# A mixture-of-experts kernel: the load of b1 moved to the head of SyncE's opening loads

## The chip, the cores and the metric

The kernel runs on one core of one Trainium2 chip. The metric is the device time of one execution in microseconds (us), so lower is better.

## The reference

Eight experts each run a two-layer network on their own 256 tokens. x is 8 x 256 x 512, w1 is 8 x 512 x 2048, w2 is 8 x 2048 x 512, all fp32; b1 is 8 x 2048 and b2 is 8 x 512.

```python
h = np.matmul(x, w1) + b1[:, np.newaxis, :]
h = np.maximum(h, 0)
return (np.matmul(h, w2) + b2[:, np.newaxis, :]).astype(np.float32)
```

## The kernel before

**Sizes and precision.** Each expert has 4 MB of w1 and 4 MB of w2 in fp32. Both are cast to fp16 by the DMAs that load them, so 2 MB of each arrive on the chip. `w1_sb` and `w2_sb` hold three experts (`NW` = 3), `xT` holds the transposed x of four (`NX` = 4), and `hT` holds the hidden layer of four (`NH` = 4).

**The two stages of the program.** First come `first_loads` and `first_turns`, whose waits are derived automatically from the data that the instructions share. Then comes a critical section, in which each engine has a program written out by hand with its own semaphores (`run_gpsimd`, `run_sync`, `run_scalar`, `run_vector`, `run_tensor`). SyncE, ScalarE, VectorE and TensorE enter the section at one wait for everything that the first stage started: the loads of both queues and the work of every engine. GpSimd passes the same wait only at line 180, after it has issued the loads of w1 of experts 1 and 2 (line 163), so those two loads lie ahead of it.

**The opening loads.** `first_loads` issues four loads from SyncE's queue (line 347) in the order of a tuple: x of expert 0 into `pair0` (512 KB), x of expert 1 into `pair1` (512 KB), b1 into `b1_rows` (64 KB, as 32 partitions of 512 fp32), and x of experts 2 and 3 into the first half of `outg0` (1 MB). GpSimd's queue gets w1 of expert 0 and b2 (line 352).

**The opening turns.** `first_turns` prepares three things:
- the identity matrix. GpSimd fills a scratch `steps` (lines 356 to 359), VectorE transposes it (line 360), and ScalarE copies four blocks into `ident` (line 363);
- the transposed x of experts 0 and 1. ScalarE casts them to fp16 (line 365), TensorE transposes them against `ident` (line 372), and ScalarE copies the result out of PSUM into `xT` (line 373);
- the transposed bias `b1T`, with four transposes on VectorE that read `b1_rows` (line 375).

On VectorE the four bias transposes are issued ahead of the transpose of `steps`, though they stand later in the source. On ScalarE the order is the two casts, the four copies into `ident`, then the two copies into `xT`.

**The critical section.** For 11 steps, TensorE runs the first layer of expert s (line 288) and then the second layer of expert s - 3 (bias at line 303, matmuls at line 318). ScalarE first casts x of experts 2 and 3 (line 195), and VectorE transposes them (line 222). ScalarE evicts the first layer with bias and ReLU (line 106); ScalarE, and VectorE for the last two experts, evict the second (line 118). SyncE waits for each load of w1 and w2 to land and then tells TensorE (lines 145 and 151). GpSimd issues the weight loads in one fixed order: w1 of expert s at line 163, then w2 of expert s - 3 at line 171, with x of experts 4 to 7 at line 177. From expert 3 on, a load waits until TensorE has finished with the buffer that it reuses. The results of experts 0 to 5 leave through GpSimd's queue (line 187), the last two through SyncE's (lines 155 and 389).

Of the kernel before, what the change touches and what calls it, by code (L numbers as in the profile page):

```python
# [10 lines left out]
def kernel(  # L11
# [20 lines left out]
    nB = P // B  # L32
# [15 lines left out]
    def sb(name, shape, dt=fp16):  # L48
        return nc.alloc_sbuf_tensor(name, shape, dt).ap()
# [10 lines left out]
    b1_rows = sb("b1rows", [E * nB, M // nB], fp32)  # L60
# [71 lines left out]
    def w1_of(e):  # L132
        return w1[e].rearrange("(p kc) m -> p kc m", kc=nKC)

    def x_of(first):
        n = FIRST[first]
        return x[first : first + n].rearrange("e (p r) h -> (e p) r h", r=n * nTB)
# [201 lines left out]

    def first_loads():  # L340
        for to, rows in (
            (x32[0], x_of(0)),
            (x32[1], x_of(1)),
            (b1_rows, b1.rearrange("e (b i) -> (e b) i", b=nB)),
            (x32[2], x_of(2)),
        ):
            tc.keep_in_program_order(nc.sync.dma_start(out=to, in_=rows))  # L347
        for to, rows in (
            (w1_sb[:, 0], w1_of(0)),
            (b2_sb, b2.rearrange("e h -> (e h)").rearrange("(o f) -> o f", o=1)),  # L350
        ):
            tc.keep_in_program_order(nc.gpsimd.dma_start(out=to, in_=rows))

    def first_turns():
# [19 lines left out]
        for b in range(nB):  # L374
            v.transpose(  # L375
                out=b1T[b * B : (b + 1) * B, nB - 1 - b : nB - 1 - b + nJ * B],
                in_=b1_rows.rearrange("r (i j) -> r j i", j=nJ))

    first_loads()
    first_turns()  # L380
    with tc.tile_critical(sync_engine=mybir.EngineType.Pool, no_gpsimd_drain=True):
# [45 lines left out]
```

## Time and profile before

| what | value |
|---|---|
| time, median of 3 runs | 180.99 us (180.72 to 181.39) |
| the profiled execution's own time | 180.8 us |
| its span, first to last instruction | 179.0 us |
| TensorE matmuls, busy | 130.6 us (73%) |
| ScalarE, busy | 86.3 us (48%) |
| VectorE, busy | 37.8 us (21%) |
| DMA, moved | 40.98 MB, mean 229 GB/s |
| HBM | read 71.39 MB, written 4.19 MB |
| landing of the b1 load after its issue | 7.5 us |

All times in the views count from the start of the span. The profiled execution took 1.8 us more than its span. DMA bytes are counted as written: a weight load that casts fp32 to fp16 reads two bytes for each byte that it moves by this count. PE is TensorE, DVE is VectorE, ACT is ScalarE, POOL is GpSimd and SP is SyncE; a trailing q names the engine's queue of commands. "x2" in a row counts instructions.

### The profile page before, as it was taken

The page shows a single profiled execution, that of the slowest core. Times are in us where ns is not written, and L with a number is a line of the kernel's source. Part 1 is how long each engine was busy: PE and PEld are TensorE (multiplying, and loading weights), DVE is VectorE, ACT ScalarE, POOL GpSimd, SP SyncE. Part 2 cuts the span into 40 slices and gives each one's busy share as a digit, 9 for nine tenths or more (in the row PEclk, how much of TensorE's full clock was granted, in tenths as well). Part 3 has the DMA queues.
Part 4 walks back from the last instruction along what each step waited for, and adds up shares of the span by engine and source line. Part 5 has one row for each costly group of instructions (what it writes and reads, how often), then busy time and mean ns, then how long its engine had stood idle before and what let it go on. Part 6 is the DMA issues. An engine that isn't in the chain of part 4 may idle for free.

```text
span 179.0 us, 2880 instructions
## 1 busy us (share of the span) xinstructions
PE 130.6 (73%) x800; PEld 86.5 (48%) x800; DVE 37.8 (21%) x39; ACT 86.3 (48%) x160; POOL 13.4 (7%) x30
## 2 busy tenths in 40 slices
PE   0004299596969993999956996699669997998940
PEld 0003278585858641786446644584268433443410
DVE  0092299300000299991000000000000000001010
ACT  3304658585858606674089705980398213121010
POOL 7100000302020101001010001000200001002000
PEclk9999999999999999579999999999999999999997
DMA  6999989999999998998999999899899999999995
GB/s 211 272 260 269 234 183 227 234 205 207 234 216 194 234 231 179 234 234 190 220 234 205 205 234 220 190 234 234 176 234 234 198 212 205 220 227 198 334 453 238
DMA packets 3825, 40.98 MB, mean 229 GB/s; under 512 B 448, under 2 KB 464, under 8 KB 1136
## 3 DMA queue, kind: packets, MB, share of 16 engines
q0 software_dynamic: 3056, 37.76, 95.2%
q1 hardware_dynamic: 768, 3.21, 4.6%
q14 instruction: 1, 0.01, 0.0%
HBM read 71.39 MB, written 4.19 MB: 422 GB/s over the span
## 4 chain that ended last, share of the span: by engine, by line
DMA 37%; PE 33%; ACT 16%; DVE 6%; issue 3%; SPq 1%; POOL 0%; ACTq 0%
PE po L318 18%; DMA w1sb<-in_w_dram 16%; PE ph L288 14%; DMA w2sb<-in_w_dram 11%; DMA outg<-in_x_dram 9%; ACT hTsb L106 8%; ACT outg L118 7%; DVE xTsb L222 6%; PE po L303 1%; ACT x L195 1%; SPq L347 1%; ACT pair L118 0%; POOL w2sb L171 0%; ACTq L422 0%; SPq L151 0%
## 5 line engine op out<-in xcount | busy, mean ns | idle before, releaser
L288 PE MATMUL ph<-xTsb,w1sb 128*128 x512 | 67.7, 291 | 23.0 <-SPq L145 7.8
L288 PEld LDWEIGHTS ph<-xTsb,w1sb 128*128 x512 | 58.5, 147 | 33.2 <-issue 30.5
L106 ACT ACTIVATE hTsb<-ph,b1T 128x256 f16<-128x256 f32 x128 | 56.8, 475 | 16.2 <-PE ph L288 15.7
L318 PE MATMUL po<-w2sb,hTsb 128*128 x256 | 56.8, 379 | 2.0 <-SPq L151 2.0
L118 ACT COPY outg<-po 32x1024 f32<-32x1024 f32 (+1 forms) x20 | 20.1, 1006 | 43.3 <-PE po L318 43.2
L318 PEld LDWEIGHTS po<-w2sb,hTsb 128*128 x256 | 24.9, 97 | 32.6 <-issue 5.1
L222 DVE STREAM_TRANSPOSE xTsb<-x 32x512 f16<-32x512 f16 (+1 forms) x32 | 31.0, 970 | 35.8 <-DMA x<-in_x_dram 28.5
L118 DVE COPY pair<-po 128x512 f32<-128x512 f32 x2 | 1.4, 692 | 88.2 <-PE po L318 88.2
L372 PE MATMUL ph<-ident,x 128*128 128x128 f16 x16 | 1.9, 310 | 15.7 <-ACT ident L363 15.7
L171 POOL DMA_DIRECT2D w2sb<-in_w_dram x10 | 5.3, 534 | 69.3 <-PE po L318 69.3
L372 PEld LDWEIGHTS <-x 128*128 128x128 f16 x16 | 1.6, 144 | 15.7 <-ACT ident L363 15.7
L163 POOL DMA_DIRECT2D w1sb<-in_w_dram x7 | 3.7, 536 | 65.8 <-PE ph L288 65.6
L118 ACT COPY pair<-po 128x512 f32<-128x512 f32 x2 | 1.2, 586 | 13.6 <-PE po L318 13.6
L375 DVE STREAM_TRANSPOSE b1T<-b1rows 32x512 f32<-32x512 f32 x4 | 4.1, 1023 | 9.3 <-DMA b1rows<-in_b_dram 9.2
L303 PE MATMUL po<-b2sb,ones 1*128 x16 | 4.8, 378 | 0.8 <-issue 0.7
L363 ACT COPY ident<-hTsb 32x32 f16<-32x32 f16 x4 | 1.0, 240 | 8.3 <-DVE hTsb L360 8.3
L365 ACT CAST x<-pair 128x1024 f16<-128x1024 f32 x2 | 2.1, 1044 | 2.3 <-DMA pair<-in_x_dram 2.3
L303 PEld LDWEIGHTS po<-b2sb,ones 1*128 1x128 f16 x16 | 1.4, 90 | 3.5 <-issue 3.2
L373 ACT COPY xTsb<-ph 128x1024 f16<-128x1024 f16 x2 | 1.9, 1014 | 1.1 <-PE ph L372 1.1
L195 ACT CAST x<-outg 128x2048 f16<-128x2048 f32 x1 | 1.9, 1900 | 0.8 <-DMA outg<-in_x_dram 0.8
L187 POOL DMA_DIRECT2D out_dram<-outg x2 | 1.1, 537 | 16.2 <-DMA w2sb<-in_w_dram 16.2
L365 ACT ACT_TABLE_LOAD x1 | 1.3, 1283 | 0.7 <-PEq L411 0.7
(12 smaller groups left out, 5.0 us busy)
## 6 DMA issues: line engine op xcount, KB each, us to landing
w1sb<-in_w_dram POOLq DMA_DIRECT2D x8, 2048.0 KB, 31.1
w2sb<-in_w_dram POOLq DMA_DIRECT2D x6, 2048.0 KB, 43.6
w2sb<-in_w_dram POOLq DMA_DIRECT2D x2, 1024.0 KB, 27.2
out_dram<-outg POOLq DMA_DIRECT2D x1, 2048.0 KB, 11.7
w2sb<-in_w_dram POOLq DMA_DIRECT2D x1, 1280.0 KB, 16.9
pair<-in_x_dram SPq DMA_DIRECT2D x2, 512.0 KB, 3.7
outg<-in_x_dram SPq DMA_DIRECT2D x1, 1024.0 KB, 16.8
x<-in_x_dram POOLq DMA_DIRECT2D x1, 1024.0 KB, 28.6
```

What stands on the lines that cost most here:

```text
L106: return nc.scalar.activation(out=to, in_=columns, func=relu_of, bias=b1T[:, at : at + 1], scale=1.0)
L118: return copy(out=t.rearrange("p (tb s) h -> p tb s h", s=split)[at : at + rows, lo:hi, k, :], in_=po[k * rows : (k + 1) * rows, e % 2, lo ...
L163: g.dma_start(out=w1_sb[:, e % NW], in_=w1_of(e)).then_inc(s_w1[e % NW], 16)
L171: g.dma_start(out=w2_sb[:, e % NW, lo:hi], in_=src[:, lo:hi]).then_inc(s_w2[e, h], 16)
L195: a.copy(out=x16[2], in_=x32[2]).then_inc(cast, 1)
L222: ins = v.transpose(out=to[b * B : (b + 1) * B, :, :, half * B : (half + 1) * B], in_=src.rearrange("p r (i kc) -> p kc r i", kc=nKC))
L288: ins = t.matmul(out=ph[i][:, 0:T], lhsT=w1_cols(w1_j, i, kc), rhs=x_cols[kc], start=(kc == 0), stop=(kc == nKC - 1),)
L303: t.matmul(out=po_f[:, bass.ds(o + tb * 512, H)], lhsT=ones1, rhs=b2_sb[0:1, bass.ds(b_e, H)], start=True, stop=False, skip_group_check=True,)
L318: ins = t.matmul(out=po_f[:, bass.ds(o + tb * 512, H)], lhsT=hT_f[:, bass.ds(h_e + (j * T + tb * P), P)], rhs=w2_f[:, bass.ds(w_e + j * H, ...
L365: a.copy(out=x16[e], in_=x32[e])
L372: t.transpose(out=to[:, kc, r, :], in_=rows[:, kc, :], identity=ident)
L375: v.transpose(out=b1T[b * B : (b + 1) * B, nB - 1 - b : nB - 1 - b + nJ * B], in_=b1_rows.rearrange("r (i j) -> r j i", j=nJ))
```

## The change

The load of b1 becomes the first of the four loads on SyncE's queue; the other three keep their order behind it. No instruction is added or removed, and the order on the other four engines stays as it was.

```diff
     def first_loads():
         for to, rows in (
+            (b1_rows, b1.rearrange("e (b i) -> (e b) i", b=nB)),
             (x32[0], x_of(0)),
             (x32[1], x_of(1)),
-            (b1_rows, b1.rearrange("e (b i) -> (e b) i", b=nB)),
             (x32[2], x_of(2)),
         ):
             tc.keep_in_program_order(nc.sync.dma_start(out=to, in_=rows))
```

## The prediction

> **What bounds the kernel now.** I read the page's DMA part first, then the chain of waits, then the opening microseconds.
>
> ```profile
> q0 software_dynamic: 3056, 37.76, 95.2%
> ```
>
> GpSimd's queue holds all the weights, and its packets fill 95.2% of the time of 16 DMA engines. The rate over the span, in stretches (last two columns: DMA share, GB/s written):
>
> ```profile
> 0.00:40.00 40.00, 18.69 (x135) 15.96 (x136) 16.59 (x21) 20.88 (x39) 5.43 (x15) 1.00 0.98 231
> 40.00:80.00 40.00, 32.63 (x221) 24.83 (x220) 18.38 (x15) 24.74 (x51) 3.19 (x6) 0.91 1.02 216
> 80.00:120.00 40.00, 32.87 (x214) 22.17 (x213) 1.41 (x2) 23.65 (x45) 1.58 (x3) 1.00 1.01 216
> 120.00:160.00 40.00, 35.25 (x190) 18.93 (x188) 0.00 (x0) 15.82 (x26) 2.11 (x4) 1.00 1.02 216
> ```
>
> The share is 0.98 to 1.02 and the rate the same 216 GB/s in three stretches, whatever PE does. Is there ever nothing queued? These are GpSimd's issues in order of time, and SyncE's marks of landings (the last columns of a mark are its start):
>
> ```profile
> 31.67 0.53 POOL L163 DMA_DIRECT2D w1sb<-in_w_dram  x1 [26.61 <-PE ph L288]
> 41.52 0.53 POOL L163 DMA_DIRECT2D w1sb<-in_w_dram  x1 [8.27 <-PE ph L288]
> 147.41 1.05 POOL L171 DMA_DIRECT2D w2sb<-in_w_dram  x2 [17.93 <-PE po L318]
> ```
> ```profile
> L145 SPq EVENT_SEMAPHORE  x1: 17/17/17, 37.1 to 37.1; - x1
> ```
> ```profile
> L145 SPq EVENT_SEMAPHORE  x1: 17/17/17, 71.1 to 71.1; - x1
> ```
> ```profile
> L151 SPq EVENT_SEMAPHORE  x2: 17/17/17, 153.5 to 158.3; - x2
> ```
>
> The w1 of expert 2, the last load issued before the section opens, lands at 37.1. The next issue, w1 of expert 3, is at 31.67, so it joins a queue that still has 5.4 us of work. The w1 of expert 4 is issued at 41.52 and lands at 71.1, 29.6 us later, of which its own 2 MiB take 9.7 at 216 GB/s: it stands behind 19.9 us of other loads. The last weights, w2 of expert 7, are issued at 147.41, while w2 of expert 6 lands until 158.3: 10.9 us to spare. So from its first packet to its last the queue is never empty. Sum: from 37.1 to the last landing lie 5 loads of w1, 8 of w2 and one of x, 27 MiB or 28.3 MB; over 131.1 us that is 216 GB/s, the rate of the stretches, with no hole left over. The last landing, from the chain in order of time:
>
> ```profile
> 71.05 0.02 SPq L145
> ...
> 147.92 20.29 DMA w2sb<-in_w_dram
> 168.22 0.02 issue
> 168.23 0.02 SPq L151
> 168.25 0.16 issue
> 168.41 3.64 PE po L318 x16
> ```
>
> What follows 168.2 is a tail of 10.8 us (16 matmuls, an eviction, the last store) that nothing in the opening touches. The chain goes through PE and ACT from 71 to 147, but only because it follows the issue of w2 of expert 7, which has those 10.9 us to spare. PE waits at both ends of that stretch, first for w1 of expert 4:
>
> ```profile
> 71.92 0.43 PE L288 MATMUL ph<-xTsb,w1sb 128*128 x1 [3.23 <-SPq L145]
> ```
> ```profile
> 168.41 3.62 PE L318 MATMUL po<-w2sb,hTsb 128*128 x16 [0.27 <-SPq L151]
> ```
>
> **The weight stream bounds the kernel**, from its start to 168.2 us.
>
> **The change, part by part.** It moves one issue on SyncE past two others. Sizes and landings after the issue, and the opening in order of time:
>
> ```profile
> pair<-in_x_dram SPq DMA_DIRECT2D x2, 512.0 KB, 3.7
> ...
> b1rows<-in_b_dram SPq DMA_DIRECT2D x1, 64.0 KB, 7.5
> b2sb<-in_b_dram POOLq DMA_DIRECT2D x1, 8.0 KB, 15.6
> ```
> ```profile
> 0.74 0.86 SPq L347 DMA_DIRECT2D pair<-in_x_dram  x2
> 1.65 0.42 SPq L347 DMA_DIRECT2D b1rows<-in_b_dram  x1
> 1.91 0.51 POOL L352 DMA_DIRECT2D b2sb<-in_b_dram  x1
> 2.12 0.42 SPq L347 DMA_DIRECT2D outg<-in_x_dram  x1
> 3.58 0.23 POOL L359 MEMSET hTsb<- 128x32 f16 x1
> 3.97 1.09 POOL L163 DMA_DIRECT2D w1sb<-in_w_dram  x2 [0.16 <-issue]
> 5.33 1.04 ACT L365 CAST x<-pair 128x1024 f16<-128x1024 f32 x1 [0.19 <-DMA pair<-in_x_dram]
> 9.22 4.13 DVE L375 STREAM_TRANSPOSE b1T<-b1rows 32x512 f32<-32x512 f32 x4 [9.22 <-DMA b1rows<-in_b_dram]
> 13.38 1.25 DVE L360 STREAM_TRANSPOSE hTsb<-hTsb 128x1024 f16<-128x1024 f16 x1
> 14.66 0.99 ACT L363 COPY ident<-hTsb 32x32 f16<-32x32 f16 x4 [8.29 <-DVE hTsb L360]
> 15.71 1.89 PE L372 MATMUL ph<-ident,x 128*128 128x128 f16 x16 [15.71 <-ACT ident L363]
> 16.79 1.93 ACT L373 COPY xTsb<-ph 128x1024 f16<-128x1024 f16 x2 [1.13 <-PE ph L372]
> 19.50 1.90 ACT L195 CAST x<-outg 128x2048 f16<-128x2048 f32 x1 [0.78 <-DMA outg<-in_x_dram]
> ```
>
> Moved forward: b1 is issued at 0.74 instead of 1.65. No row shows b1 alone on the queue. From above, a load of 512 KB at the head took about 3.7 us (the median of the two x); from below it takes nothing after its issue, 0.42. The nearest row is the x load, so I take 3.7: b1 lands at 4.4 instead of 9.2. VectorE's queue then runs 4.13 us of b1 transposes to 8.6, the transpose of `steps` (its last fill ends at 3.8, in time) to 9.8, ScalarE's 0.99 to about 10.9, PE's 1.89, and the copies end 1.1 us after PE, at about 13.9 instead of 18.72. So **this chain gains 4.8 us** (about 8 at the lower end).
>
> What is late next: the entry into the section. ScalarE's first instruction there is the cast at 19.50, and the chain gives what released it:
>
> ```profile
> 2.12 16.84 DMA outg<-in_x_dram
> 18.96 0.02 issue
> ```
>
> That is x of experts 2 and 3, landing at 18.96, just 0.24 us after the copies. Its issue stays at 2.12, as the four issues fill the same slots. Behind it stands b2: 1.91 + 15.6 = 17.5 us, on GpSimd's queue behind w1 of expert 0. So the entry can move from 18.98 to 17.5 at best, 1.5 us, and only if x of 2 and 3 lands sooner. It might: b1 took 7.5 us for 64 KB in the midst of the weights, where x took 3.7 for 512 KB ahead of them, and in after b1 no longer stands in front of it there. Bounds for the entry: 17.5, and a slip by the 0.42 us of one issue with as much again for a turn, say 19.8. Neither reaches the end: 1.5 us earlier means that expert 3's w1 joins the queue with 6.9 us to spare, 0.8 us later with 4.6, and in both cases PE waits for w1 of expert 4 at 71.1. So **the 4.8 us end as waiting**, first at the entry and then at 71.1: worth 0.
>
> Moved back: the two x loads by one issue, 0.42 us. The cast of the second moves from 5.33 to about 5.8 and ends at 6.8, while ScalarE's next, the copies into `ident`, waits until 9.8: 3 us of cover. If the second x is caught by the weights and takes b1's 7.5 us, it is cast at 9.1 to 10.1 and the chain slips 0.3 us, under the same cover at the entry.
>
> What is not covered is the stream's own start. Half-microsecond stretches of the opening:
>
> ```profile
> 2.00:2.50 0.50, 0.00 (x0) 0.00 (x0) 0.00 (x0) 0.02 (x1) 0.50 (x2) 1.00 0.61 205
> 2.50:3.00 0.50, 0.00 (x0) 0.00 (x0) 0.00 (x0) 0.00 (x0) 0.50 (x1) 1.00 1.05 385
> ...
> 4.00:4.50 0.50, 0.00 (x0) 0.00 (x0) 0.00 (x0) 0.40 (x1) 0.50 (x1) 1.00 1.02 418
> ```
>
> From 2.5 on the engines are full, at about 400 GB/s of unconverted x. With b1 in front they have 64 KB to do in the 0.42 us before x arrives: 64 KB at 400 GB/s is 0.16 us, so they lose 0.42 - 0.16 = **0.26 us** that the stream never gets back, since the bytes to move are the same. Bounds: 0 (the engines are not full before 2.5 anyway) and 0.42 (b1's 32 partitions are slow). I take 0.26.
>
> Sum on the profiled execution: 180.8 - 0 + 0.26 = 181.06. That execution lies 0.19 under the median, 180.99; on the median the sum is 181.25, and **I predict 181.2 us**. Differences under 0.5%, 0.9 us, count as no change here, about what a measurement of this kernel can tell.
>
> **The rivals.**
>
> *Faster: the earlier entry reaches the end.* Price: the 1.5 us from 18.98 to 17.5, so 179.5. For it: the chain of waits does begin with the load of x of experts 2 and 3. Against it: the 5.4 us and 10.9 us of queue, and PE's wait of 3.23 us. Chance 0.08.
>
> *Slower: VectorE's b1 transposes starve GpSimd's queue.* They move from 9.22 to about 4.4, and lie beside the issue at 3.97 of w1 of experts 1 and 2 and the start of w1 of expert 0. If GpSimd cannot prepare transfers while VectorE transposes, the stream halts for up to 4.13 us. SyncE's x of experts 2 and 3 covers 1 MB at 400 GB/s, 2.6 us; what is left, 1.5 us, goes to the end: 182.7. It decides once the halt is over 2.6 us. Against it: GpSimd's issue at 31.67 takes 0.53 beside VectorE's transposes, as the one at 41.52 without. Chance 0.12.
>
> The Trainium skill (SBUF — State Buffer, "SBUF: two separate sides") says that VectorE in a two-port mode keeps GpSimd from writing descriptors, so that the DMA engines sit idle; "Who interferes with whom" there exempts one-input instructions outside those modes. By the first this rival holds, by the second it costs nothing; the 0.53 beside transposes agrees with the second, but no row shows a landing that had no slack.
>
> *The stream runs at another rate.* How the 16 engines fall in step could change with the order of the first loads. 1% of the 131.1 us is 1.3 us: 182.3, or 179.7. The three runs of before lie within 0.67 us, which speaks against swings of that size. Chance 0.08 for slower, 0.03 for faster.
>
> *The change does not bring b1 in sooner*, because the landing is set by something other than its place. Then only the order of issues moves: 181.0. Chance 0.05.
>
> **How the numbers follow.** My forecast has 0.64, so 181.2 is the likeliest. Faster by over 0.5% holds 0.08 + 0.03 = 0.11. Slower by over 0.5% holds 0.12 + 0.08 = 0.20. The rest, 0.64 + 0.05 = 0.69, is no change. The forecast's own range is 180.6 (no loss, and 0.4 of spread of the runs) to 181.8 (0.42 lost, and the same spread). For 8 in 10 it reaches up to the dearest slower case, 182.7, and down a little, to 180.2; the faster cases, 0.11, stay out.
>
> **What would show it.** In the trace after: b1 transposes at 3 to 4.5, PE's transposes at 10 to 12 instead of 15.71; ScalarE's cast of x of 2 and 3 still released by a DMA, at 18 to 20; expert 4's matmuls still waiting for line 145 near 71.3; the last matmuls released near 168.5. I am wrong if PE no longer waits at 71, if w1 of expert 2 lands over 1 us away from 37.1 (then the opening changed the stream), or if a stretch after 40 us leaves 216 GB/s.

## The result, and the profile after

The change made the kernel slower: 185.48 us (median of 6 runs, 185.01 to 186.91) against 180.71 us (6 runs), a ratio of 1.0266 with a 95% interval of 1.0246 to 1.0286. That is 4.8 us. The profiled execution took 185.57 us, with a span of 183.8 against 179.0 us. I forecast 181.2 in a range of 180.2 to 182.7. Two of the four runs of casts_3_w2_ahead, at 185.6 us, had a lower granted clock (0.942) than every other run (0.952 or more) and are left out below.

The opening of the changed kernel, in order of time (start, duration, what; in brackets the idle time of the engine before it and what ended it):

```profile
0.74 0.39 SPq L347 DMA_DIRECT2D b1rows<-in_b_dram  x1
1.19 0.89 SPq L347 DMA_DIRECT2D pair<-in_x_dram  x2
1.25 0.67 POOL L352 DMA_DIRECT2D w1sb<-in_w_dram  x1 [0.80 <-POOLq L411]
...
2.56 4.14 DVE L375 STREAM_TRANSPOSE b1T<-b1rows 32x512 f32<-32x512 f32 x4 [2.56 <-DMA b1rows<-in_b_dram]
...
4.50 1.04 ACT L365 CAST x<-pair 128x1024 f16<-128x1024 f32 x1 [2.48 <-DMA pair<-in_x_dram]
...
16.83 1.04 ACT L365 CAST x<-pair 128x1024 f16<-128x1024 f32 x1 [11.29 <-DMA pair<-in_x_dram]
...
18.83 1.90 PE L372 MATMUL ph<-ident,x 128*128 128x128 f16 x16 [18.83 <-ACT ident L363]
...
28.23 1.90 ACT L195 CAST x<-outg 128x2048 f16<-128x2048 f32 x1 [6.39 <-DMA outg<-in_x_dram]
...
29.84 9.25 PE L288 MATMUL ph<-xTsb,w1sb 128*128 x64 [9.11 <-SPq L145]
...
39.39 0.53 POOL L163 DMA_DIRECT2D w1sb<-in_w_dram  x1 [34.33 <-PE ph L288]
```

b1 does come early: VectorE starts on it at 2.56 instead of 9.22. But the second x load, cast at 5.33 before, is now cast at 16.83, and ScalarE idles 11.29 us for it. It was issued only 0.44 us later (1.6 against 1.18). Behind it in the same queue, x of experts 2 and 3 slips as well (cast at 28.23 against 19.50), the section is entered at 27.9, and TensorE's first matmul of expert 0 stands at 29.84 instead of 21.11, 8.7 us late. The 16 transposes for x come at 18.83 instead of 15.71: b1 was ahead of time, and the chain later.

The trace also holds every packet of the DMA engines; here a packet is one row of a load, and each x load has 128 rows, eight on each of 16 engines. The weights' first row on an engine starts at 3.91 to 4.70 in the changed kernel, when the first x is through, and every row of the second x comes behind it. In before it starts at 4.66 to 4.98, when the second x is through as well. GpSimd's issue stands at 1.25 in both; why the same issue takes effect 0.75 us sooner is not shown.

What became of the weight stream? Stretches of the changed kernel (last two columns: DMA share and GB/s written), the long ones first:

```profile
0.00:40.00 40.00, 10.96 (x80) 9.31 (x80) 14.99 (x19) 15.29 (x26) 4.47 (x14) 1.00 0.89 212
40.00:80.00 40.00, 33.17 (x242) 25.86 (x242) 15.04 (x14) 24.90 (x52) 4.16 (x8) 1.00 1.00 210
80.00:120.00 40.00, 32.20 (x196) 21.37 (x196) 6.34 (x6) 22.89 (x43) 1.58 (x3) 0.96 1.01 216
```
```profile
37.00:38.00 1.00, 0.93 (x9) 0.88 (x9) 0.99 (x2) 0.75 (x3) 0.00 (x0) 1.00 0.09 16
38.00:39.00 1.00, 1.00 (x10) 0.85 (x8) 0.97 (x3) 1.00 (x3) 0.00 (x0) 1.00 0.00 0
39.00:40.00 1.00, 0.09 (x1) 0.00 (x0) 0.99 (x2) 0.60 (x2) 0.61 (x2) 1.00 0.00 0
```

Between 37 and 40 us the DMA engines stand still. Expert 3's w1 reuses a buffer that TensorE must first be done with, and its issue came at 39.39, after the queue had run dry. SyncE's marks of landings show what became of the stream: w1 of expert 2 first, w1 of expert 3 next, the last weights at the end.

```profile
L145 SPq EVENT_SEMAPHORE  x1: 17/17/17, 38.5 to 38.5; - x1
```
```profile
L145 SPq EVENT_SEMAPHORE  x1: 17/17/17, 51.8 to 51.8; - x1
```
```profile
L151 SPq EVENT_SEMAPHORE  x1: 17/17/17, 173.0 to 173.0; - x1
```

At 9.7 us for 2 MiB, 38.5 leads to 48.2; 51.8 is 3.6 us more. The last weights land 4.8 us later than in before (168.2). And TensorE? Its waits in the changed kernel, longest first (in total, times, longest), and below them those of before for weights (lines 145 and 151) and for ScalarE's evictions (line 106):

```profile
PE ph L372 <- ACT ident L363: 18.8, 1, 18.8
PE ph L288 <- ACT hTsb L106: 10.2, 4, 2.6
PE ph L288 <- SPq L145: 10.0, 2, 9.1
PE ph L288 <- issue: 6.8, 6, 1.8
PE po L303 <- issue: 0.9, 5, 0.2
```
```profile
PE ph L288 <- SPq L145: 7.8, 4, 3.2
...
PE ph L288 <- ACT hTsb L106: 4.9, 3, 2.0
PE po L318 <- SPq L151: 2.0, 3, 1.1
```

No wait for w2 (line 151) is left, and those for w1 come to 10.0 us, 9.1 of them the entry. From 29.84 to the end TensorE waits for weights for 0.9 us, where it waited 9.8 in before; its waits for ScalarE's evictions have doubled, from 4.9 to 10.2. All three signs of being wrong that I had named are there: no wait for weights near 71, w1 of expert 2 landing 1.4 us late, and a stretch after 40 us at 210 GB/s. Two things are late at once, the weight stream by 4.8 us and TensorE by its start, and the trace alone does not say which of them is the price.

### The profile page after: what moved, and what is told of

Its sections match the earlier page's. It is cut to its first block, busy times and chain, and to the rows that moved or that the text cites. A ratio compares the mean times of both kernels' runs of the same rounds, so it can differ in the third digit from the quotient of the medians.

```text
span 183.8 us, 2880 instructions
## 1 busy us (share of the span) xinstructions
PE 130.5 (71%) x800; PEld 87.1 (47%) x800; DVE 37.8 (21%) x39; ACT 86.0 (47%) x160; POOL 13.4 (7%) x30
## 4 chain that ended last, share of the span: by engine, by line
PE 54%; ACT 24%; DMA 14%; issue 4%; POOL 1%; SPq 0%; POOLq 0%
PE po L318 31%; PE ph L288 21%; ACT hTsb L106 15%; DMA w1sb<-in_w_dram 14%; ACT outg L118 9%; PE po L303 2%; POOL hTsb L356 1%; POOL w1sb L352 0%; ACT pair L118 0%; POOL b2sb L352 0%; POOL ones L358 0%; POOL hTsb L359 0%; POOL ident L357 0%; SPq L145 0%; POOLq L411 0%
## 5 line engine op out<-in xcount | busy, mean ns | idle before, releaser
L288 PE MATMUL ph<-xTsb,w1sb 128*128 x512 | 67.9, 293 | 28.1 <-ACT hTsb L106 10.2
L106 ACT ACTIVATE hTsb<-ph,b1T 128x256 f16<-128x256 f32 x128 | 56.7, 474 | 16.0 <-PE ph L288 15.2
L318 PE MATMUL po<-w2sb,hTsb 128*128 x256 | 56.6, 379 | 0.0
L360 DVE STREAM_TRANSPOSE hTsb<-hTsb 128x1024 f16<-128x1024 f16 x1 | 1.2, 1245 | 0.0
## 6 DMA issues: line engine op xcount, KB each, us to landing
out_dram<-outg POOLq DMA_DIRECT2D x1, 2048.0 KB, 11.5
```

Of the source, the lines that this page charges most:

```text
L106: return nc.scalar.activation(out=to, in_=columns, func=relu_of, bias=b1T[:, at : at + 1], scale=1.0)
L288: ins = t.matmul(out=ph[i][:, 0:T], lhsT=w1_cols(w1_j, i, kc), rhs=x_cols[kc], start=(kc == 0), stop=(kc == nKC - 1),)
L318: ins = t.matmul(out=po_f[:, bass.ds(o + tb * 512, H)], lhsT=hT_f[:, bass.ds(h_e + (j * T + tb * P), P)], rhs=w2_f[:, bass.ds(w_e + j * H, ...
```

## The experiments

Theory A: the second x is overtaken by the weights, packet by packet, so the section is entered late. For the way from there to the end it has two forms. A1: the hole in the weight stream sets the end. A2: TensorE has nothing left to give up. Theory B: VectorE's early bias transposes hinder GpSimd's loads. Theory C: b1's transfer of 32 partitions upsets the queue in which it stands.

### Which event holds up the second x

**b1_on_act.** b1 as early, from another queue.

```diff
+        tc.keep_in_program_order(nc.scalar.dma_start(
+            out=b1_rows, in_=b1.rearrange("e (b i) -> (e b) i", b=nB)))
         for to, rows in (
-            (b1_rows, b1.rearrange("e (b i) -> (e b) i", b=nB)),
             (x32[0], x_of(0)),
```

> The load of b1 is issued from ScalarE's queue at the start; x of experts 0 and 1 are issued from SyncE at 0.74 and 1.2 us, as in before. Theory A (the second x is overtaken by the weights because it starts one issue later): the second x lands near 5.3 us as in before, the section is entered by 19 us, and the time is 180.7 us, within 0.9 us. Theory B (VectorE's early bias transposes hinder GpSimd's loads): the transposes run early here too, so about 185.5 us. Theory C (b1's 32-partition transfer upsets the queue that it stands in): about 181 us, since b1 has a queue of its own.

Measured: 181.04 us, ratio 1.0019 (1.0010 to 1.0029). Its opening:

```profile
4.05 4.15 DVE L376 STREAM_TRANSPOSE b1T<-b1rows 32x512 f32<-32x512 f32 x4 [4.05 <-DMA b1rows<-in_b_dram]
...
5.98 1.04 ACT L366 CAST x<-pair 128x1024 f16<-128x1024 f32 x1 [0.22 <-DMA pair<-in_x_dram]
...
10.56 1.89 PE L373 MATMUL ph<-ident,x 128*128 128x128 f16 x16 [10.56 <-ACT ident L364]
...
21.05 10.31 PE L288 MATMUL ph<-xTsb,w1sb 128*128 x64 [8.60 <-issue]
```

With b1 early and x in time, TensorE's transposes come 5.2 us sooner (10.56 against 15.71), and the first matmul of expert 0 at 21.05, as in before. So an early b1 alone gains nothing and costs little (0.34 us). Theory B falls: the transposes lie beside GpSimd's issues here too, and in after the first weights came earlier than in before, not later.

**one_row_first.** The order of before, with one row of b1 split off and put in front.

```diff
+            (b1_rows[0:1], b1.rearrange("e (b i) -> (e b) i", b=nB)[0:1]),
             (x32[0], x_of(0)),
             (x32[1], x_of(1)),
-            (b1_rows, b1.rearrange("e (b i) -> (e b) i", b=nB)),
+            (b1_rows[1:], b1.rearrange("e (b i) -> (e b) i", b=nB)[1:]),
```

> The order of before, but one row of b1 (2 KB) is a load of its own at the head of SyncE's queue; the other 31 rows stay in third place. So x is issued one issue later, with hardly any bytes ahead of it, and the bias transposes stay late. Theory A: the second x lands after 14 us as in after, the rest of b1 behind it near 19 us, and the chain of turns starts only then: the section is entered at about 30 us and the time is 186 to 190 us. Theory B: about 181 us. Theory C (the 64 KB in front, not the time): about 181 us.

Measured: 206.05 us, ratio 1.1409 (1.1390 to 1.1428).

```profile
15.87 1.04 ACT L366 CAST x<-pair 128x1024 f16<-128x1024 f32 x1 [10.31 <-DMA pair<-in_x_dram]
```
```profile
37.43 4.13 DVE L376 STREAM_TRANSPOSE b1T<-b1rows 32x512 f32<-32x512 f32 x4 [37.43 <-DMA b1rows<-in_b_dram]
...
49.00 9.51 PE L288 MATMUL ph<-xTsb,w1sb 128*128 x64 [3.18 <-issue]
```

Only 2 KB in front, and the second x is cast at 15.87: it is the place in time that counts, not b1's 64 KB. Theory C, which gave 181 us here, falls. The size of the loss I missed by 16 us, since the other 31 rows of b1 landed at 37.4 and not near 19.

**w1_1us_later.** The changed kernel, with one more fill on GpSimd ahead of the first weights.

```diff
+        tc.keep_in_program_order(nc.gpsimd.memset(hT[:, 0, 0:4, :], 0.0))
         for to, rows in (
             (w1_sb[:, 0], w1_of(0)),
```

> The changed kernel with one more fill of 1 us on GpSimd ahead of its first load, so that the first weights start 1 us later. Theory A: both x loads are through before the weights start, the second x lands by 6.5 us, the section is entered by 20 us, and the time is 180.7 to 182 us though one engine was given more to do. Theory B: the bias transposes still lie beside GpSimd's issues, 185 us or more. Theory C: 185 us or more.

Measured: 181.10 us, ratio 1.0023 (1.0013 to 1.0033).

```profile
1.63 0.67 POOL L353 DMA_DIRECT2D w1sb<-in_w_dram  x1
...
2.66 4.16 DVE L376 STREAM_TRANSPOSE b1T<-b1rows 32x512 f32<-32x512 f32 x4 [2.66 <-DMA b1rows<-in_b_dram]
...
6.02 1.04 ACT L366 CAST x<-pair 128x1024 f16<-128x1024 f32 x1 [0.27 <-DMA pair<-in_x_dram]
...
21.15 10.43 PE L288 MATMUL ph<-xTsb,w1sb 128*128 x64 [10.07 <-issue]
```

The fill hid partly behind other work, so the weights were issued only 0.38 us later, at 1.63. That was enough: by the packet records their first row starts at 5.28, when both x are through, the second x is cast at 6.02, and the whole loss but 0.4 us is gone, with b1 in front and the bias transposes as early as in after. This shows the cause of the late entry: **a race of the second x with the first weights, decided by some 0.4 us.**

**w1_less_later.** The same with three quarters of the fill (`hT[:, 0, 0:3, :]`).

> As w1_1us_later, but with a fill of three quarters, so that the first weights are issued near 1.4 us, between the 1.25 of after and the 1.63 of w1_1us_later. Gradual (each row of the second x that is still to come when the weights start costs one turn of 1.5 us): three to five of its eight rows are caught, it lands at 9 to 12 us, the section is entered at 20 to 24 us, 181 to 182.5 us. All or nothing: either as w1_1us_later, 181.1 us with the second x by 6.5 us, or as after, 185.5 us with the second x near 17 us.

Measured: 182.18 us (181.91 to 184.37), ratio 1.0078 (1.0042 to 1.0113). The profiled execution, at 184.23 one of its longer ones, issued the weights at 1.41 and cast the second x at 15.26, with the first matmul at 27.37. Three of the ten executions took 183.9 to 184.4 us, the other seven 181.9 to 182.4, so 0.22 us of issue time decides the race, and not the same way each time. In the profiled execution 57 of the second x's 128 rows came behind the weights, against all of them in after and none in w1_1us_later. Its part on each engine was complete at 6.5 us on one, at 8.9 on another, between 10.1 and 11.5 on thirteen, and at 14.9 on the last. So the gradual form holds on each engine by itself, and the load lands with the slowest of 16, later than the 9 to 12 us that I expected. What decides when the weights reach an engine stays open.

**b1_second.** The order is x of expert 0, b1, x of expert 1.

```diff
-            (b1_rows, b1.rearrange("e (b i) -> (e b) i", b=nB)),
             (x32[0], x_of(0)),
+            (b1_rows, b1.rearrange("e (b i) -> (e b) i", b=nB)),
             (x32[1], x_of(1)),
```

> The order is x of expert 0, b1, x of expert 1, x of experts 2 and 3: the first x starts as in before, the second as late as in after. Theory A (the second x is overtaken because its issue at 1.6 us is one issue too late): it lands after 14 us, the section is entered near 28 us, 185.5 us. Rival (what counts is when the first x is through, since the two x share the queue): the second x lands within 9 us, and the time is 181 us.

Measured: 187.01 us (186.28 to 188.97), ratio 1.0338 (1.0301 to 1.0374). The second x was cast at 18.57 and the first matmul came at 32.02. An early first x does not help; b1 ahead of the second x does the damage from there too, and 1.5 us more than expected.

**w1_in_quarters.** The changed kernel, with w1 of expert 0 in four loads, whose rows write 4 KB and not 16 KB.

```diff
-            (w1_sb[:, 0], w1_of(0)),
+            *((w1_sb[:, 0, kc], w1_of(0)[:, kc]) for kc in range(nKC)),
```

> The changed kernel, with w1 of expert 0 loaded as four loads of a quarter each, so that a row of the load writes 4 KB and not 16 KB. Theory A with turns (each packet of x waits for one packet of the weights on its DMA engine): the weights' packet takes a quarter, about 0.3 us, eight turns of the second x take some 4 us instead of 12, it lands by 9 us, the section is entered by 20 us and the time is within 0.9 us of 180.7. Rival (the second x waits until the first load of weights as a whole is through): it lands at 15 us or later, 185 us.

Measured: 181.91 us, ratio 1.0070 (1.0052 to 1.0088).

```profile
9.01 1.04 ACT L365 CAST x<-pair 128x1024 f16<-128x1024 f32 x1 [3.51 <-DMA pair<-in_x_dram]
...
21.30 9.90 PE L288 MATMUL ph<-xTsb,w1sb 128*128 x64 [8.40 <-issue]
```

The second x is in time, though the 181.91 us lie 0.3 above what I had allowed. The packet records give the price of a row. In after a row of weights takes 1.226 us and a row of x 0.172, and the rows of the second x on an engine start 1.375 us apart (5.12, 6.50, 7.87 and so on). With rows of a quarter a row of weights takes 0.322 us, and those of x start about 0.49 apart. Eight such turns are 11.0 and 3.9 us. So each row of x waits for one row of weights: the mechanism, by its size. The Trainium skill (DMA: Bandwidth & Descriptors, "Queues, rings and completion order") says that each DMA engine goes round its queues and drains a whole packet of one before it switches; from the weights' first row on, the two spacings agree with that.

### How a late entry reaches the end

**w2_ahead** and **x4_ahead** fill the hole, each with a load that GpSimd issues before the section's wait.

```diff
             if step == NW - 1:
+                load_w2(0)
                 tc.wait_critical_data_deps()
-            if step >= LAG:
+            if step > LAG:
```
```diff
-                if step == 4:
-                    g.dma_start(out=x16[step], in_=x_of(step)).then_inc(s_x, 16)
...
             if step == NW - 1:
+                g.dma_start(out=x16[4], in_=x_of(4)).then_inc(s_x, 16)
                 tc.wait_critical_data_deps()
```

> The changed kernel, but GpSimd issues w2 of expert 0 before the section's wait instead of after w1 of expert 3, so the weight stream has 2 MB more queued while the section is late. The second x still lands near 17 us and the section is still entered near 28 us. Theory A1 (the end is late because the weight stream ran dry, 3.6 of the 4.8 us): the hole is gone, 181 to 182.5 us. Theory A2 (the end is late because TensorE starts 8.7 us later and has no longer any wait to give up): 185.5 us, within 0.7 us.

> The changed kernel, but GpSimd issues the load of x of experts 4 to 7 (1 MB written, 4.9 us at 216 GB/s) before the section's wait, in place of w2 of expert 0 in w2_ahead. It fills the hole of 3.6 us in the weight stream and delays w1 of expert 3 less (landing near 53 us, before TensorE asks for it at 61). Theory A1 (the hole sets the end): 181 to 182.5 us. Theory A2 (TensorE's late start sets it, the hole or none): 185.4 us, within 0.7 us.

Measured: 185.18 us, ratio 1.0235 (1.0208 to 1.0263), and 184.40 us, ratio 1.0205 (1.0181 to 1.0230). The stretch from 36 to 42 us of after, w2_ahead and x4_ahead:

```profile
36.00:42.00 6.00, 4.17 (x37) 3.71 (x36) 5.53 (x8) 3.81 (x10) 1.58 (x3) 1.00 0.40 63
```
```profile
36.00:42.00 6.00, 4.13 (x37) 3.68 (x35) 4.72 (x7) 3.77 (x9) 1.07 (x2) 1.00 1.01 216
```
```profile
36.00:42.00 6.00, 4.17 (x37) 3.72 (x36) 4.55 (x7) 3.81 (x9) 1.07 (x2) 1.00 1.01 208
```

The hole is gone in both (216 and 208 GB/s against 63), the loss of time is not. Theory A1 falls as the price of this change. x4_ahead lies 0.3 us below the range given for A2; its first matmul, at 28.84 and so 1.0 us earlier than in after, accounts for most of the 1.1 us that it took less.

**casts_3, casts_6** leave the loads of before alone and delay the entry with three or six repeated casts on ScalarE; **casts_3_x4_ahead** and **casts_3_w2_ahead** add the fillers.

```diff
             a.copy(out=xT[:, e], in_=pt.rearrange("p (kc t) -> p kc t", kc=nKC))
+        for _ in range(3):
+            a.copy(out=x16[1], in_=x32[1])
```

> The kernel before, with three casts of x of expert 1 repeated on ScalarE (3.1 us in all) ahead of the section, whose wait waits for them. The loads are as in before. The section is entered near 21.9 us, 2.9 us later. Theory A2 (TensorE, once started, needs 154 us to the end of the span; in before it starts at 21.1 and so has 179.0 - 21.1 - 154.0 = 3.9 us to give up): no change, 180.7 us within 0.9. Theory A1 (5.4 us of queue to spare): the same.

> As casts_3, but with six casts, 6.3 us: the section is entered near 25 us, 6.0 us later. Theory A2: 6.0 - 3.9 = 2.1 us are lost, 182.8 us (181.9 to 183.7, as the first expert's matmuls vary by 1 us). Theory A1 (5.4 us of queue): 0.6 us, 181.3 us.

> casts_3 (the kernel before, entered 3.1 us later) with x of experts 4 to 7 issued before the section's wait. Nothing is held up behind it: w1 of expert 3 lands near 52 us and is asked for at 55.9. If the 1.0 us that casts_3 lost is the hole in the weight stream: 180.7 to 181.0 us. If TensorE has less than 3.1 us to give up: 181.6 us.

> The kernel before with both edits: three repeated casts (the section is entered 3.1 us later) and w2 of expert 0 issued before the section's wait. In casts_3 the third load of the section was issued 3.0 us before the queue ran dry and yet landed 1.0 us late. Theory A1 (that 1.0 us is a hole in the weight stream, since a load needs some 4 us from its issue to its first data): the hole is filled, 180.7 to 181.0 us. Theory A2 alone (TensorE has less to give up than the 3.9 us worked out): 181.6 us, as casts_3.

Measured: casts_3 181.62 us, ratio 1.0052 (1.0034 to 1.0070); casts_6 184.42, ratio 1.0199 (1.0181 to 1.0217); casts_3_x4_ahead 180.92, ratio 1.0007 (0.9990 to 1.0024). Issue and landing of w1 of expert 3 in casts_3, then the first matmuls of casts_3_x4_ahead:

```profile
34.30 0.53 POOL L163 DMA_DIRECT2D w1sb<-in_w_dram  x1 [29.24 <-PE ph L288]
```
```profile
L145 SPq EVENT_SEMAPHORE  x1: 17/17/17, 48.0 to 48.0; - x1
```
```profile
25.26 10.33 PE L287 MATMUL ph<-xTsb,w1sb 128*128 x64 [6.44 <-issue]
```

casts_3 lost about 1 us where both forms said none. Its w1 of expert 2 landed at 37.3, so that of expert 3, issued 3.0 us before, was due at 47.0; it landed at 48.0. That is no hole in the stream as a whole: from 36 to 40 us it moved 193 GB/s, against 197 in before.

```profile
36.00:40.00 4.00, 3.84 (x34) 3.38 (x33) 0.00 (x0) 3.31 (x8) 0.00 (x0) 1.00 0.93 193
```
```profile
36.00:40.00 4.00, 3.88 (x34) 3.43 (x33) 0.00 (x0) 3.52 (x9) 0.00 (x0) 1.00 0.93 197
```

The difference is about one row of 16 KB. A load has landed with the last of its 16 parts, one on each DMA engine. Of w1 of expert 3, fifteen parts were complete by 46.98 and the last at 47.95; in before all were between 46.50 and 46.80. One part stays as late to the last weights: fifteen by 168.18, the last at 169.15. So a microsecond that one engine loses delays every later landing. Why it lost it is not shown. With the filler the loss is gone, though TensorE starts 4.1 us later than in before: so TensorE had about 4 us to give up.

casts_3_w2_ahead does not decide between its forms: 182.65 and 183.56 us, both above what either gave, because w2 in front held w1 of expert 3 back to 56.6 us, where TensorE waited 4.5 us for it. casts_6 lost 3.8 us where I expected 2.1: its first matmul came 6.4 us later than in before, not 6.0, and TensorE needed 154.9 us from there, not 154.0.

The first matmul and the span of each profile, side by side:

| kernel | first matmul of expert 0 | span | from one to the other |
|---|---|---|---|
| before | 21.11 | 179.0 | 157.9 |
| b1_on_act | 21.05 | 179.3 | 158.3 |
| w1_1us_later | 21.15 | 179.4 | 158.3 |
| w1_in_quarters | 21.30 | 179.7 | 158.4 |
| casts_3 | 24.19 | 179.9 | 155.7 |
| casts_3_x4_ahead | 25.26 | 179.3 | 154.0 |
| w1_less_later | 27.37 | 182.4 | 155.0 |
| casts_6 | 27.49 | 182.4 | 154.9 |
| x4_ahead | 28.84 | 182.5 | 153.7 |
| w2_ahead | 29.02 | 183.9 | 154.9 |
| after | 29.84 | 183.8 | 154.0 |
| b1_second | 32.02 | 187.2 | 155.2 |
| one_row_first | 49.00 | 203.3 | 154.3 |

Whatever the reason for a late start, TensorE needs 153.7 to 155.2 us from its first matmul to the end once it hardly waits for weights. Up to a start near 25 us the weight stream sets the end, at 179 to 180 us; beyond it the start does. That is A2. By this spread TensorE had 157.9 less 153.7 to 155.2, so 2.7 to 4.2 us, to give up in before; of after's 8.7 us of delay that leaves 4.5 to 6.0, and the span grew by 4.8. None of the versions is faster than the kernel before.

## Why the prediction was wrong

- **"The weight stream bounds the kernel"** was right for before, but I took it for more: TensorE stood only some 3 to 4 us behind it. I read PE's waits, 3.23 us at 71.9 and a short one at the end, as proof that PE did not matter. Nor is their sum the reserve: of the 9.8 us of waits for weights in before 0.9 are left in after, but 5.3 have come back as waits for ScalarE.
- **"This chain gains 4.8 us", worth 0** was right where both x are in time: TensorE's transposes come 5.2 us sooner in b1_on_act and 6.5 in w1_1us_later (9.19), and nothing of it reaches the end.
- **The step that failed is the cover of the moved x loads.** I wrote that the second x, if it "is caught by the weights and takes b1's 7.5 us", is cast at 9.1 to 10.1. It was caught, and cast at 16.83, 15.2 us after its issue. b1's 64 KB have two rows for each of 16 engines, x has eight, and every row waits for a row of weights, eight turns of 1.375 us: the 7.5 us of a small load were no bound for a larger one.
- **"Bounds for the entry: 17.5 ... 19.8"** failed with it: 27.9. I allowed "as much again for a turn", 0.42 us. In front of x of experts 2 and 3 stood the second x's eight turns, 11.0 us, in place of b1's two. The cover behind the entry was reckoned for a slip of 0.8 us at most, and 8.7 came.
- **"5.4 us of work" in the queue** as reserve was too much: with 3.0 us left in casts_3 one engine already fell behind, and 1.0 us was lost.
- **The 0.26 us lost at the stream's start** did not come about in after, where the weights' first row started earlier than in before. In b1_on_act and w1_1us_later it started at 5.21 and 5.28, against 4.66, and they took 0.34 and 0.40 us more than before: the sign and the size fit, but neither run tests 64 KB in front of x by itself.
- **The slower rival, starved GpSimd,** had the right side and the wrong mechanism. The bias transposes lie at 2.66 in w1_1us_later, between the issue of the first weights at 1.63 and their first row at 5.28, without harm to the time. Of the two rules of the Trainium skill, these runs agree with the one in "Who interferes with whom" (SBUF — State Buffer), that one-input instructions outside the two-port modes do not hinder GpSimd.
- **"Faster: the earlier entry reaches the end"** had nothing to work with, as the entry came later. Where it could have come earlier, in b1_on_act and w1_1us_later, ScalarE's first cast in the section still stands at 19.33 and 19.42, released by b2.

## What to carry to other kernels

A load at the head of a shared queue moves every load behind it, and what counts is not the issue time that it costs but whether the loads behind still get through before a stream of large rows from another queue begins. Price a transfer inside such a stream by its rows on each engine times one row of the stream, not by the landing time of a smaller neighbour. And do not take the waits of the second-busiest chain for its reserve, since one wait gives way to another: here 9.8 us of waits for weights were 3 to 4 us of reserve, and runs that only delayed its start found it.

## What the runs showed of the hardware that was not expected

- A shift of 0.38 us in the issue of the weights (after and w1_1us_later) moved the landing of a 512 KB load by 11 us.
- Beside a stream whose rows take 1.226 us, each row of x, 0.172 us by itself, came 1.375 us after the one before it (after).
- In one_row_first, 31 rows of b1 (62 KB) took from the landing of the second x, 15.9 us, to 37.4 us, where 32 rows took 3.9 us behind it in before (cast at 5.33, transposed at 9.22). The Trainium skill (DMA: Bandwidth & Descriptors, "Why a DMA increments its semaphore by 16 and not by 1") says that a load is spread over the largest number of engines, up to 16, that divides its rows: 16 for 32 rows, one for 31. The trace agrees: the 31 rows came one after another, never two at once, 16 times with 1.30 us from one to the next, where the 32 rows in before came in two rounds of 16.
- One of 16 parts of a load that fell 1.0 us behind kept the landings of the stream about 1.0 us late, to the last one 120 us on (casts_3).
